# A decoder layer in split fp32: two-term products in three 256-column matmuls, one-operation evictions, and a larger padding tile

## The chip, the cores and the metric

The kernel runs on one core of a Trainium2 chip. The metric is the device time of one execution in microseconds; the time of a kernel is the median of its runs. The engines are TensorE (PE, matmuls; PEld is its weight loads), VectorE (DVE), ScalarE (ACT), GpSimd (POOL) and SyncE (SP, which issues most DMAs).

## What is computed

One layer of a hybrid decoder over 256 tokens of width 2048, all in fp32. In short:

```python
h = rms_norm(x, attn_norm_g)
proj = h @ w_in                                   # 2048 -> 4448 columns
y_rwkv = rwkv7_mixer(token_shift(proj[:3360]))    # 16 heads x 64, recurrent
y_mla = mla_mixer(proj[3360:])                    # 8 heads of latent attention
x = x + concat(y_rwkv, y_mla) @ w_out
h = rms_norm(x, ffn_norm_g)
gate = causal_conv3(h @ w_gate) + conv_b          # 2048 -> 5632
x = x + (silu(gate) * (h @ w_up)) @ w_down        # 5632 -> 2048
return rms_norm(x, final_norm_g)
```

## The kernel before

**Split operands.** TensorE is fed with a rounded format. To come near fp32, each operand is cut into a rounded high part (hi) and what the rounding left over (lo). A product is the sum of three parts: hi x hi, hi x lo and lo x hi. Weights come from memory in pieces of 128 x 1024 fp32. `piece` (L125) issues the DMA of one from SyncE into a tile raw, ScalarE copies it, rounded, into hi (L133), and VectorE subtracts hi from raw into lo (L134). There are three buffers each for raw, hi and lo.

**Two kinds of products.** In `prod_b` (L162) the weights are stationary and the activations stream. The activation tiles, x (four tiles, x_65 to x_68 in the lists below) for the input projection, z for gate and up, cl for the up-projections of the attention, hold for each slice of 128 input channels the high parts of the 256 tokens and behind them their low parts, 512 columns in all. For the eight slices of a piece, one matmul with the high weights runs over all 512 columns (L165): columns 0 to 255 of the accumulator get hi x hi, columns 256 to 511 get the high weights times the low activations. Then eight matmuls with the low weights (L168) add lo x hi into columns 0 to 255. Two pieces fill an accumulator (a tile mm in PSUM, 128 x 512 fp32). In the attention's up-projections a product takes four slices of a piece in place of eight. One call of `prod_b` with eight slices is called a half product below.

In `prod_a` (L178) the activations are stationary and 512 weight columns stream, with three matmuls per slice (L185 to L187). It serves the output projection (stationary tile yhi), the down projection (stationary tiles hh and hl) and the attention's values. The change does not touch it.

**Eviction.** `joined` (L172) empties an accumulator of `prod_b`: ScalarE copies its second half to the destination (L173), VectorE adds the first half (L174), and VectorE multiplies by the row of reciprocal norms, rsB or its like (L175), which the norm has left until then. The destination is h, kraw, gt, up or another tile of the caller.

**Order of the work.** The input projection (35 accumulators of 128 output columns) is mixed with the work of the recurrent mixer: as each pair of accumulators is ready, the kernel appends what depends on them, the gram matrices (pg, L527), transposes (pt, L547), and a triangular solve on VectorE (L578 to L584) that first loads a tile Lp by DMA. Then follow the recurrence in chunks and the attention, the output projection, and from about 466 us to the end the feed-forward layer, in two blocks: for each of 44 column tiles a gate and an up product (L957 to L976), and after each block the down projection. The program order is written by hand, but a scheduler goes over it with an estimate of each instruction's duration and sets the order in each engine's queue. Each engine works through its queue in order. The accumulators mm have three buffers, as have the accumulators ch of the mixer. A tile takes its place in SBUF in the order in which it is allocated; `pad` and `pad2` are tiles that nothing reads.

Of the kernel before, what the change touches and what calls it, by code (L numbers as in the profile page):

```python
# [14 lines left out]
ALU = mybir.AluOpType  # L15
AX = mybir.AxisListType

P = 128
T = 256
# [35 lines left out]
def hybrid_layer(ctx: ExitStack, tc: tile.TileContext, a: dict, out: bass.AP):  # L55
    nc = tc.nc
    V, S, PE = nc.vector, nc.scalar, nc.tensor
# [24 lines left out]
    def hl4(n):  # L82
        return a8(n).rearrange("p (k s) t -> p k s t", s=2)
# [10 lines left out]
    def mm(n="mm"):  # L94
        return ps.tile([P, 512], F32, tag="mm", name=nm(n), bufs=NMM)
# [7 lines left out]
    def con(shape, n, dt=F32):  # L103
        return sb.tile(shape, dt, name=n, bufs=1)
# [2 lines left out]
    nc.gpsimd.memset(pad, 0.0)  # L107
    xT = a["xT"]
    xs_ = [hl4("x") for _ in range(4)]
    pad2 = con([P, 8], "pad2")  # L110
    nc.gpsimd.memset(pad2, 0.0)
    vec = con([P, NVEC], "vec")
    cst = con([P, NCST], "cst")
# [48 lines left out]
    def prod_b(acc, pieces, act, kt0, n, first, last):  # L162
        hi, lo = pieces
        for j in range(n):
            PE.matmul(acc, hi[:, j * P:(j + 1) * P], act(kt0 + j), start=first and j == 0, stop=False,  # L165
                      skip_group_check=True)
        for j in range(n):
            PE.matmul(acc[:, :T], lo[:, j * P:(j + 1) * P], act(kt0 + j)[:, 0, :], start=False,  # L168
                      stop=last and j == n - 1, skip_group_check=True)


    def joined(dst, acc, scale, rows=slice(0, P)):  # L172
        S.copy(dst, acc[rows, T:])  # L173
        V.tensor_tensor(dst, acc[rows, :T], dst, ALU.add)  # L174
        V.tensor_tensor(dst, dst, scale[rows], ALU.mult)  # L175


    def prod_a(accs, pieces, act_hi, act_lo, kt0, n, first, last, tbs=(0, 1)):  # L178
# [12 lines left out]
    def in_tile(i, pf=mm):  # L191
        acc = pf()
        for h in range(2):
            eng = nc.gpsimd if h and 17 <= i < 25 else None
            prod_b(acc, piece(a["win"][i, h], eng=eng), x_hl, h * 8, 8, h == 0, h == 1)
        flush()
        return acc
# [121 lines left out]
    with tc.manual_schedule(engines={mybir.EngineType.SP}):  # L319
        for g in range(4):  # L320
            xsplit(g)
            if g == 0:
                nc.scalar.dma_start(cst, a["cst"])
            if g % 2 == 0:
                for i in range(2):
                    pcs[i, g // 2] = piece(a["win"][wt0[i], g // 2])
            for i in range(2):
                hl = tuple(u[:, (g % 2) * 512:(g % 2 + 1) * 512] for u in pcs[i, g // 2])
                prod_b(acc0[i], hl, x_hl, g * 4, 4, g == 0, g == 3)
        for h in range(2):  # L330
            prod_b(acc0[2], piece(a["win"][26, h]), x_hl, h * 8, 8, h == 0, h == 1)
        sums(0)
        kacc[0] = in_tile(1)
        dve0 = last_lo[0]
        sums(1)
        kacc[1] = in_tile(2, ch)
        rope_tables()
        lora = s4(n="lora")
        nc.sync.dma_start(lora, a["lora"])
# [32 lines left out]
    def shifted(acc, i, rows=slice(0, P), dst=None):  # L372
        h = t1("h", 257)
        nc.gpsimd.memset(h[rows, 0:1], 0.0)
        joined(h[rows, 1:257], acc, rsB, rows)
        o = t1("sh") if dst is None else dst
        S.activation(o[rows], h[rows, 1:257], AF.Copy, scale=om_mu[rows, i:i + 1])
        V.scalar_tensor_tensor(o[rows], h[rows, 0:256], vv("mu", i, rows), o[rows], ALU.mult, ALU.add)
        return o
# [50 lines left out]
    acc = acc0[2]  # L430
    kraw, ksw = t1("kraw"), t1("ksw")
    joined(kraw[0:64], acc, rsB, slice(0, 64))
    shifted(acc, 26, rows=slice(64, 96), dst=sg2)
    sigmoid_(sg2, slice(64, 96))
# [12 lines left out]
    for p in range(8):  # L447
# [4 lines left out]
        acc = kacc[p] if p in kacc else in_tile(1 + p)  # L452
# [45 lines left out]
    for p in range(8):  # L498
        pp, g = p // 2, p % 2
        acc = in_tile(9 + p)  # L500
# [256 lines left out]
    def latent(x, gname, post):  # L757
        c_ = [s4(F32R, "cl").rearrange("p (k s t) -> p k s t", k=2, s=2) for _ in range(2)]
        ssum = t2("css")
        for j in range(4):  # L760
            acc = in_tile(27 + x * 4 + j)
            cr = t2("cr")
            joined(cr, acc, rsB)
            if j == 0:
                S.activation(ssum, cr, AF.Square)
            else:
                sq = t2("csq")
                S.activation(sq, cr, AF.Square)
                V.tensor_tensor(ssum, ssum, sq, ALU.add)
            h_, l_ = (c_[j // 2][:, j % 2, q, :] for q in range(2))  # L770
            S.activation(h_, cr, AF.Copy, scale=vv(gname, j))
            V.scalar_tensor_tensor(l_, cr, vv(gname, j), h_.bitcast(F32), ALU.mult, ALU.subtract)
        pss = at("pss")
        for tb in range(2):
            PE.matmul(pss[:, tb * 2:tb * 2 + 2], ssum[:, tb * P:(tb + 1) * P], ones[:, 0:2], start=True, stop=True)
        m = st("ssm", 2)
        V.tensor_copy(m, pss[:, 0:4:2])
        rr = con([P, 2], f"rr{x}")
        V.tensor_scalar(rr, rsqrt(m, 1.0 / 512, EPS, 2), post, None, ALU.mult)
        rb = con([P, T], f"rrB{x}")  # L780
        bcast(rr, rb, at, t2)
        rrs.append(rr)
        rrB.append(rb)
        cl.append(c_)
# [167 lines left out]
    for blk, nf in enumerate((24, 20)):  # L952
        hh = [s4(F32R, "hh").rearrange("p (k t) -> p k t", k=4) for _ in range(nf // 4)]
        hl = [s4(F32R, "hl").rearrange("p (k t) -> p k t", k=4) for _ in range(nf // 4)]
        for fi in range(nf):
            f = f0 + fi
            accs = []  # L957
            for gu in range(2):
                acc = mm()
# [24 lines left out]
        n = nf // 2  # L984
# [105 lines left out]
```

## Time and profile before

| | |
|---|---|
| Time, median of 3 runs | 1208.7 us (1208.7, 1202.65, 1214.32) |
| Profiled execution: span | 1203.6 us, 18439 instructions (the page has no other time for it) |
| TensorE busy | 1159.9 us (96%) in 6993 matmuls |
| its weight loads | 990.6 us (82%) |
| VectorE busy | 839.1 us (70%) |
| ScalarE busy | 599.4 us (50%) |
| GpSimd busy | 77.4 us (6%) |
| DMA | 215.82 MB, mean 179 GB/s |

The busy times are shares of the span. Matmuls are pipelined and their ends are modelled, so the pace of TensorE is read from the starts of successive matmuls or from long runs of them, not from the busy time. The chain that the profile follows back from the last instruction names what was waited for at each step; windows give the busy time of each engine in a stretch of the span. In both, "L165" is a line of the kernel, an arrow points from what is read to what is written, and "x8" is a count of instructions.

### The profile page before, as it was taken

To read this page: it belongs to the slowest core of one execution; us is meant where nothing else is said; L and a number is where in the kernel's file an instruction comes from. 1 tells how busy PE (TensorE), PEld (TensorE's weight loads), DVE (VectorE), ACT (ScalarE), POOL (GpSimd) and SP (SyncE) were. 2 spreads that over 40 slices of the span, in tenths; PEclk is the share of its full clock that TensorE was granted. 3 is DMA by queue.
4 is the path that set the end of the run, shared out by engine and by line. 5 is a ranking of instruction groups with operands and counts; after the bars stand their busy time and mean duration, and the time that the engine had idled before them with its cause. 6 is when DMAs were issued, how large, how long until landed. Compare 5 with 4: busy or idle time off the path is not lost.

```text
span 1203.6 us, 18439 instructions
## 1 busy us (share of the span) xinstructions
PE 1159.9 (96%) x6993; PEld 990.6 (82%) x6993; DVE 839.1 (70%) x1352; ACT 599.4 (50%) x939; POOL 77.4 (6%) x214
## 2 busy tenths in 40 slices
PE   7899998998799999999999999999999999999996
PEld 6788877887577888888888888888888888888885
DVE  6898749977887556777777776444577777775563
ACT  6784434633444455655555554333455555554442
POOL 1500042002110001000000000000000000000000
PEclk9899998999999999999999999999999999999999
DMA  8555443754133555655555555555655555566662
GB/s 317 177 155 159 138 143 122 213 168 147 62 140 114 184 172 175 206 190 191 187 192 191 191 192 191 193 190 190 200 191 192 192 193 193 192 223 202 205 217 81
DMA packets 71017, 215.82 MB, mean 179 GB/s; under 512 B 17616, under 2 KB 17872, under 8 KB 70928
## 3 DMA queue, kind: packets, MB, share of 16 engines
q1 hardware_dynamic: 69776, 211.84, 53.9%
q10 hardware_dynamic: 768, 2.05, 0.5%
q8 instruction: 55, 0.90, 0.3%
q0 software_dynamic: 384, 0.75, 0.2%
q14 instruction: 34, 0.28, 0.1%
HBM read 210.48 MB, written 3.41 MB: 178 GB/s over the span
## 4 chain that ended last, share of the span: by engine, by line
PE 84%; DVE 8%; DMA 3%; POOL 2%; issue 1%; ACT 1%; SPq 1%; ACTq 0%; DVEq 0%; POOLq 0%
PE mm L165 34%; PE mm L168 17%; PE mm L185 9%; PE mm L187 9%; PE mm L186 9%; DVE lo L134 2%; PE pg L527 1%; DMA xt<-in_x 1%; PE px L677 1%; DMA Lp<-dL 1%; DMA raw<-in_win 0%; POOL cosR L291 0%; DMA dT<-Tq 0%; PE py L677 0%; SPq L540 0%
## 5 line engine op out<-in xcount | busy, mean ns | idle before, releaser
L134 DVE TENSOR_TENSOR lo<-raw,hi 128x1024 fp32r<-128x1024 f32 x368 | 453.0, 1231 | 288.0 <-ACT hi L133 283.1
L133 ACT CAST hi<-raw 128x1024 fp32r<-128x1024 f32 x376 | 395.5, 1052 | 451.7 <-issue 234.9
L165 PE MATMUL mm<-z,hi 128*128 128x512 f32 x1408 | 351.3, 392 | 0.0
L165 PEld LDWEIGHTS mm<-z,hi 128*128 128x128 f32 x1408 | 251.9, 188 | 43.7
L168 PEld LDWEIGHTS mm<-z,lo 128*128 128x128 f32 x1408 | 188.3, 188 | 14.5
L168 PE MATMUL mm<-z,lo 128*128 128x256 f32 x1408 | 191.6, 278 | 0.0
L165 PE MATMUL mm<-x,hi 128*128 128x512 f32 x528 | 144.4, 410 | 17.9 <-DVE h L174 9.6
L186 PE MATMUL mm<-lo,hh 128*128 128x512 f32 x336 | 130.7, 389 | 0.0
L187 PE MATMUL mm<-hi,hl 128*128 128x512 f32 x336 | 130.7, 389 | 0.0
L165 PEld LDWEIGHTS mm<-x,hi 128*128 128x128 f32 x528 | 97.0, 195 | 35.6 <-ACT hi L133 8.3
L185 PE MATMUL mm<-hi,hh 128*128 128x512 f32 x336 | 119.7, 389 | 0.0
L168 PEld LDWEIGHTS mm<-x,lo 128*128 128x128 f32 x528 | 74.7, 193 | 7.4 <-issue 1.0
L168 PE MATMUL mm<-x,lo 128*128 128x256 f32 x528 | 79.9, 288 | 0.0
L186 PEld LDWEIGHTS mm<-lo,hh 128*128 128x128 f32 x336 | 63.1, 188 | 13.1
L187 PEld LDWEIGHTS mm<-hi,hl 128*128 128x128 f32 x336 | 63.1, 188 | 13.1
L185 PEld LDWEIGHTS mm<-hi,hh 128*128 128x128 f32 x336 | 63.1, 188 | 13.0
L186 PE MATMUL mm<-lo,yhi 128*128 128x512 f32 x128 | 51.1, 399 | 0.0
L187 PE MATMUL mm<-hi,ylo 128*128 128x512 f32 x128 | 50.5, 394 | 0.0
L185 PE MATMUL mm<-hi,yhi 128*128 128x512 f32 x128 | 49.6, 405 | 0.0
L964 POOL MEMSET gt<- 128x2 f32 x44 | 4.3, 100 | 575.8 <-DVE hl L976 558.9
L187 PEld LDWEIGHTS mm<-hi,ylo 128*128 128x128 f32 x128 | 24.1, 188 | 5.6 <-DVE ylo L749 0.4
L185 PEld LDWEIGHTS mm<-hi,yhi 128*128 128x128 f32 x128 | 23.9, 188 | 5.7 <-DVE kn L174 0.8
(291 smaller groups left out, 1142.8 us busy)
## 6 DMA issues: line engine op xcount, KB each, us to landing
raw<-in_wgu SPq DMA_DIRECT2D x176, 512.0 KB, 3.3
raw<-in_wdn SPq DMA_DIRECT2D x88, 512.0 KB, 4.1
raw<-in_win SPq DMA_DIRECT2D x70, 512.0 KB, 3.7
raw<-in_wout SPq DMA_DIRECT2D x32, 512.0 KB, 3.4
raw<-in_wuq SPq DMA_DIRECT2D x6, 512.0 KB, 3.3
xraw<-in_xT SPq DMA_DIRECT2D x4, 512.0 KB, 6.3
xt<-in_x SPq DMA_DIRECT2D x4, 512.0 KB, 6.7
raw<-in_wuv SPq DMA_DIRECT2D x4, 512.0 KB, 3.3
```

The lines of the kernel that those rows point to most:

```text
L133: S.copy(hi, raw)
L134: sub = (eng or V).tensor_tensor(lo, raw, hi.bitcast(F32), ALU.subtract).ins
L165: PE.matmul(acc, hi[:, j * P:(j + 1) * P], act(kt0 + j), start=first and j == 0, stop=False, skip_group_check=True)
L168: PE.matmul(acc[:, :T], lo[:, j * P:(j + 1) * P], act(kt0 + j)[:, 0, :], start=False, stop=last and j == n - 1, skip_group_check=True)
L185: PE.matmul(accs[tb], ah, wh, start=first and j == 0, stop=False)
L186: PE.matmul(accs[tb], ah, wl, start=False, stop=False)
L187: PE.matmul(accs[tb], al, wh, start=False, stop=last and j == n - 1)
L527: PE.matmul(pg[h][:, o:o + P], BK[pp][hs, gg, w * 2 + r, :, :], AR[pp][hs, gg, w * 2 + r, :, :], start=o == 0, stop=True, skip_group_check ...
L677: PE.matmul(dst[HS[h], a_ * 64:(a_ + 1) * 64], lhsT, rhs, start=n == 0 and a_ == 0, stop=True, skip_group_check=True)
L964: nc.gpsimd.memset(gt[:, 0:2], 0.0)
```

## The change

`prod_b` now runs two matmuls of 256 columns for each slice with the high weights, one over the high and one over the low activations, and both add into columns 0 to 255, as the matmuls with the low weights do. The same high weights are thus loaded twice. `joined` has one operation left: VectorE multiplies the accumulator by the reciprocal norms into the destination. There are 144 such evictions, 88 of them of gate and up. `pad2` grows from 8 to 88 fp32 per partition, from 32 to 352 bytes: each tile that is allocated after it moves by 320 bytes, while the x tiles (whose buffers z uses later) and `pad` stay. The two products of a slice carry no `skip_group_check` any more, which is no instruction.

```diff
-    pad2 = con([P, 8], "pad2")
+    pad2 = con([P, 88], "pad2")
...
         for j in range(n):
-            PE.matmul(acc, hi[:, j * P:(j + 1) * P], act(kt0 + j), start=first and j == 0, stop=False,
-                      skip_group_check=True)
+            for s in range(2):
+                PE.matmul(acc[:, :T], hi[:, j * P:(j + 1) * P], act(kt0 + j)[:, s, :],
+                          start=first and j == 0 and s == 0, stop=False)
         for j in range(n):
             PE.matmul(acc[:, :T], lo[:, j * P:(j + 1) * P], act(kt0 + j)[:, 0, :], start=False,
-                      stop=last and j == n - 1, skip_group_check=True)
+                      stop=last and j == n - 1)
...
     def joined(dst, acc, scale, rows=slice(0, P)):
-        S.copy(dst, acc[rows, T:])
-        V.tensor_tensor(dst, acc[rows, :T], dst, ALU.add)
-        V.tensor_tensor(dst, dst, scale[rows], ALU.mult)
+        V.tensor_tensor(dst, acc[rows, :T], scale[rows], ALU.mult)
```

Lines behind the eviction thus stand one line higher than before, and the two loops of `prod_b` one lower (L166 and L169). In the lists below a row is a run of like instructions in an engine's queue: line, operation, tile written, tiles read, shape and count.

TensorE, one half product of an accumulator of gate and up and the next one, before:

```order
L165 MATMUL mm_5616<-z_4387,hi_5641 128x512 x4
L165 MATMUL mm_5616<-z_4388,hi_5641 128x512 x4
L168 MATMUL mm_5616<-z_4387,lo_5642 128x256 x4
L168 MATMUL mm_5616<-z_4388,lo_5642 128x256 x4
L165 MATMUL mm_5678<-z_4385,hi_5681 128x512 x4
L165 MATMUL mm_5678<-z_4386,hi_5681 128x512 x4
L168 MATMUL mm_5678<-z_4385,lo_5682 128x256 x4
L168 MATMUL mm_5678<-z_4386,lo_5682 128x256 x4
```

The same place on TensorE after the change:

```order
L166 MATMUL mm_6221<-z_4915,hi_6254 128x256 x8
L166 MATMUL mm_6221<-z_4916,hi_6254 128x256 x8
L169 MATMUL mm_6221<-z_4915,lo_6255 128x256 x4
L169 MATMUL mm_6221<-z_4916,lo_6255 128x256 x4
L166 MATMUL mm_6295<-z_4913,hi_6298 128x256 x8
L166 MATMUL mm_6295<-z_4914,hi_6298 128x256 x8
L169 MATMUL mm_6295<-z_4913,lo_6299 128x256 x4
L169 MATMUL mm_6295<-z_4914,lo_6299 128x256 x4
```

A half product is 24 matmuls of 256 columns where it was 8 of 512 and 8 of 256; nothing else stands between them.

VectorE at the beginning of the solve (about 178 us in the profile before; Lp is the solve's matrix, Mp its mask, Tq its result, tm a temporary, h the destination of an eviction), before:

```order
L134 TENSOR_TENSOR lo_2040<-raw_2037,hi_2039 128x1024
L134 TENSOR_TENSOR lo_2093<-raw_2090,hi_2092 128x1024
L578 TENSOR_TENSOR Lp_1766<-Lp_1766,Mp 128x1024
L582 TENSOR_TENSOR tm_1822<-Tq_1821,Lp_1766 128x31
L584 TENSOR_TENSOR Tq_1821<-Tq_1821,tm_1822 128x31
L174 TENSOR_TENSOR h_1904<-mm_1776,h_1904 128x256
L582 TENSOR_TENSOR tm_1822<-Tq_1821,Lp_1766 128x60
L175 TENSOR_TENSOR h_1904<-h_1904,rsB 128x256
```

The same place on VectorE after the change:

```order
L134 TENSOR_TENSOR lo_2284<-raw_2281,hi_2283 128x1024
L577 TENSOR_TENSOR Lp_2046<-Lp_2046,Mp 128x1024
L134 TENSOR_TENSOR lo_2360<-raw_2357,hi_2359 128x1024
L581 TENSOR_TENSOR tm_2116<-Tq_2115,Lp_2046 128x31
L174 TENSOR_TENSOR h_2198<-mm_2054,rsB 128x256
L583 TENSOR_TENSOR Tq_2115<-Tq_2115,tm_2116 128x31
L174 TENSOR_TENSOR h_2274<-mm_2213,rsB 128x256
```

The solve's first multiply stands one split (lo) earlier, and the next eviction follows it behind that split, one operation long.

TensorE between the last matmul of the gram matrices and the accumulator that waits at that place (pv are transposes of the mixer), before:

```order
L165 MATMUL mm_1974<-x_66,hi_1977 128x512 x4
L168 MATMUL mm_1974<-x_65,lo_1978 128x256 x4
L168 MATMUL mm_1974<-x_66,lo_1978 128x256 x4
L165 MATMUL mm_1974<-x_67,hi_1999 128x512
L615 MATMUL pv_1912<-cst,sh_1773 128x128 x2
L165 MATMUL mm_1974<-x_67,hi_1999 128x512 x3
L165 MATMUL mm_1974<-x_68,hi_1999 128x512 x4
L168 MATMUL mm_1974<-x_67,lo_2000 128x256 x4
L168 MATMUL mm_1974<-x_68,lo_2000 128x256 x4
L165 MATMUL mm_2036<-x_65,hi_2039 128x512 x4
```

The same place on TensorE after the change:

```order
L614 MATMUL pv_2204<-cst,sh_2051 128x128 x2
L166 MATMUL mm_2213<-x_65,hi_2216 128x256 x8
L166 MATMUL mm_2213<-x_66,hi_2216 128x256 x8
L169 MATMUL mm_2213<-x_65,lo_2217 128x256 x4
L169 MATMUL mm_2213<-x_66,lo_2217 128x256 x4
L166 MATMUL mm_2213<-x_67,hi_2246 128x256 x8
L166 MATMUL mm_2213<-x_68,hi_2246 128x256 x8
L169 MATMUL mm_2213<-x_67,lo_2247 128x256 x4
L169 MATMUL mm_2213<-x_68,lo_2247 128x256 x4
L166 MATMUL mm_2280<-x_65,hi_2283 128x256 x8
L166 MATMUL mm_2280<-x_66,hi_2283 128x256 x8
L169 MATMUL mm_2280<-x_65,lo_2284 128x256 x4
```

Ahead of the waiting accumulator (mm_2036 before, mm_2356 after) stand the second half of mm_1921 and all of mm_1974 before, and the rest of mm_2054 and all of mm_2213 and mm_2280 after.

## The prediction

> **What bounds the kernel now.** First the page's span and busy times, then the chain that ended last (its line by engine and its line by source line).
>
> ```profile
> span 1203.6 us, 18439 instructions
> PE 1159.9 (96%) x6993; PEld 990.6 (82%) x6993; DVE 839.1 (70%) x1352; ACT 599.4 (50%) x939; POOL 77.4 (6%) x214
> PE 84%; DVE 8%; DMA 3%; POOL 2%; issue 1%; ACT 1%; SPq 1%; ACTq 0%; DVEq 0%; POOLq 0%
> PE mm L165 34%; PE mm L168 17%; PE mm L185 9%; PE mm L187 9%; PE mm L186 9%; DVE lo L134 2%; PE pg L527 1%; DMA xt<-in_x 1%; PE px L677 1%; DMA Lp<-dL 1%; DMA raw<-in_win 0%; POOL cosR L291 0%; DMA dT<-Tq 0%; PE py L677 0%; SPq L540 0%
> ```
>
> TensorE carries 84% of the chain, and L165 and L168, the two lines that the change rewrites, half of it. VectorE carries 8%. Busy time by stage says where:
>
> ```profile
> core 0: us, PE busy (x) PEld busy (x) DVE busy (x) ACT busy (x) POOL busy (x), PEclk, DMA share, GB/s
> 40.00:50.00 10.00, 7.41 (x25) 6.27 (x26) 7.05 (x14) 6.77 (x13) 8.06 (x25) 0.66 0.52 163
> 50.00:88.00 38.00, 37.55 (x222) 31.21 (x221) 37.29 (x84) 33.35 (x63) 1.31 (x10) 1.00 0.48 142
> 178.00:200.00 22.00, 15.99 (x82) 13.71 (x82) 18.68 (x39) 11.50 (x23) 5.06 (x5) 0.84 0.39 138
> 265.00:375.00 110.00, 95.58 (x957) 76.39 (x956) 89.60 (x166) 46.52 (x99) 17.29 (x46) 0.98 0.31 107
> 466.00:1180.00 714.00, 714.00 (x3832) 616.85 (x3831) 477.78 (x651) 357.04 (x508) 8.87 (x58) 1.00 0.59 194
> ```
>
> From 466 us on (gate, up and down) TensorE is never idle and VectorE has a third of its time free: an eviction saved there is worth nothing, a nanosecond per matmul everything. VectorE is nearly full from 50 to 88 us, and TensorE loses time at 40 to 50, 178 to 200 and 265 to 375 us.
>
> **The change, part 1: three matmuls of 256 columns for one of 512 and one of 256.** The chain in the gate/up stage, in order of time, gives the pace:
>
> ```profile
> 695.18 1.83 PE mm L165 x8
> 697.01 0.94 PE mm L168 x8
> 697.96 1.83 PE mm L165 x8
> 699.79 0.91 PE mm L168 x8
> ...
> 706.21 1.83 PE mm L165 x8
> ```
>
> Four half products (8 matmuls of L165 and 8 of L168 each) take 706.21 - 695.18 = 11.03 us, 2.7575 us each. There are 176 (1408 matmuls of L165 on z, by eights). Each becomes 24 matmuls of 256 columns, so all depends on the pace of those. A 512-column matmul takes 1.83/8 = 229 ns. A 256-column one takes 0.91/8 = 114 or 0.94/8 = 117.5 ns, in turns. Two halves thus cost 228 to 235 ns: the second load of the high half buys and costs almost nothing beside a full stream. Whether it is made at all, lines 185 and 186 tell: there one stationary operand (yhi or hh) serves two matmuls in a row, and both have their weight load.
>
> ```profile
> L186 PEld LDWEIGHTS mm<-lo,hh 128*128 128x128 f32 x336 | 63.1, 188 | 13.1
> L185 PEld LDWEIGHTS mm<-hi,hh 128*128 128x128 f32 x336 | 63.1, 188 | 13.0
> ```
>
> Which pace will a long run take? The padding tile moves every tile behind x and z by 320 bytes. In the built program x and z begin 160 bytes past a multiple of 512, hi and lo 352 bytes past one; after the change all of them are at 160. Now only the up-projections (tile cl, at 352 as hi and lo are) read both operands from the same offset. Their 256-column runs are four long:
>
> ```profile
> 315.58 1.09 PE L165 MATMUL mm<-cl,hi 128*128 128x512 f32 x4
> 316.50 0.64 PE L168 MATMUL mm<-cl,lo 128*128 128x256 f32 x4
> 316.98 1.09 PE L165 MATMUL mm<-cl,hi 128*128 128x512 f32 x4
> ...
> 329.65 0.63 PE L168 MATMUL mm<-cl,lo 128*128 128x256 f32 x4
> 330.12 1.08 PE L165 MATMUL mm<-cl,hi 128*128 128x512 f32 x4
> ```
>
> By starts, four take 316.98 - 316.50 = 0.48 and 330.12 - 329.65 = 0.47 us, in the mean 118.75 ns each, slower than either pace on z. I take this, since it is the only row with the placement that z will have. A half product then takes 24 x 118.75 ns = 2.850 us, +0.0925 us; x176 = **+16.3 us**. The bounds are the fastest and slowest rows: 24 x 0.91/8 = 2.730 us, -4.8 us in all, and 24 x 0.48/4 = 2.880 us, +21.6 us.
>
> [...]
>
> The input projection has 70 half products on x, which in the stage where TensorE waits least take
>
> ```profile
> 104.97 0.94 PE mm L168 x8
> 105.91 1.84 PE mm L165 x8
> 107.75 0.94 PE mm L168 x8
> ```
>
> 107.75 - 104.97 = 2.78 us. At 2.850 that is +0.07 us each. Some 14 of them run between 40 and 88 us, where VectorE's full queue hides it; 56 x 0.07 = **+3.9 us** (-2.8 to +5.6 by the same bounds; all 70 if that cover is gone, +1). The 20 up-projection products go from 316.98 - 315.58 = 1.40 to 12 x 118.75 = 1.425 us: **+0.5 us** (-0.7 to +0.8).
>
> **Part 2: the padding and the 512-column matmuls that stay.** In the output projection's second half the stationary tile yhi stands at 160 and hi and lo at 352; in the down projection hh stands at 352 like them.
>
> ```profile
> 447.38 0.39 PE L186 MATMUL mm<-lo,yhi 128*128 128x512 f32 x1
> ...
> 448.54 0.39 PE L185 MATMUL mm<-hi,yhi 128*128 128x512 f32 x1
> 789.63 0.39 PE L186 MATMUL mm<-lo,hh 128*128 128x512 f32 x1
> ...
> 790.76 0.62 PE L185 MATMUL mm<-hi,hh 128*128 128x512 f32 x2
> ```
>
> Five steps take 1.16 and 1.13 us: 232 against 226 ns. With all at 160, the 192 matmuls of that half should step at 226: **-1.2 us** (0 if offset is not the reason).
>
> **Part 3: one operation per eviction.** joined loses a copy on ScalarE and an add on VectorE, 144 times:
>
> ```profile
> L174 DVE TENSOR_TENSOR gt<-mm,gt 128x256 f32<-128x256 f32 x44 | 18.4, 419 | 0.0
> L173 ACT COPY gt<-mm 128x256 f32<-128x256 f32 x44 | 16.1, 367 | 0.0
> ```
>
> The 88 of gate and up are hidden under TensorE: nothing. The weight DMAs stay as many, and their queue has room (DMA share 0.59 from 466 us on). Elsewhere:
>
> - 40 to 88 us: 10 adds of 0.42 us, 4.2 us of a full VectorE queue. I take **-3** (0 to -4.2): TensorE, 37.55 of 38 us busy behind it, is late next.
> - The wait at 178 us. VectorE's queue holds the solve's first multiply (line 578), which waits for a DMA, ahead of the eviction that frees the accumulator. First the chain, then TensorE's rows:
>
> ```profile
> 175.82 6.07 DMA Lp<-dL
> 181.92 1.24 DVE Lp L578
> 183.66 0.34 DVE h L174
> 177.32 0.73 PE L168 MATMUL mm<-x,lo 128*128 128x256 f32 x5
> 184.05 3.78 PE L165 MATMUL mm<-x,hi 128*128 128x512 f32 x8 [6.01 <-DVE h L174]
> ```
>
>  In the new order two whole tiles and most of a third stand between the last gram matmul and the blocked tile, where one and three quarters stood: some 6 us more to do. But VectorE now has a split (lo, 1.23 us) between that multiply and the eviction. And behind the 6.01 us of idling eight matmuls took 3.78 us in place of 1.83, at a granted clock of 0.84. So 6 - 6 + 1.2 leaves a wait of 1 to 2 us and no lost clock. I take **-5** (+1.2 if only the split counts, -8 with all the clock's 2 us).
> - 265 to 375 us: 22 adds, 9.2 us of VectorE's 89.6. TensorE lacks 14.4 us there, partly to chains without an eviction (the scan, group norm). I take **-4** (0 to -9.2).
>
> [...]
>
> **Sum.** 16.3 + 3.9 + 0.5 - 1.2 - 3 - 5 - 4 = +7.5 us on the profiled span of 1203.6, 1211.1 us. The page has no other time for that execution; the median of the runs, 1208.7, lies 5.1 us above its span. With it the forecast is **1216 us**, +0.6%. About 1% (12 us) is what a measurement of this kernel can tell from no change.
>
> **The rivals.**
>
> - *The run locks at the fast pace.* z's rows hold 0.91 for eight matmuls on end, every second time; without a 512-column run to throw them off, they may all do so. For it: eight are a longer run than four. Against it: z's offset then is not z's offset now. -4.8 - 2.8 - 0.7 - 1.2 - 12 = -21.5: **1187 us**.
> - *The paces go on in turns,* (0.91 + 0.94)/16 = 115.6 ns, 2.775 us: +3.1 us, 0 in front, -1.2 - 12: **1199 us**.
> - *The weight load becomes the bound* (the slower side). With 256 columns there is one load per 119 ns or so; if loads slow each other, matmuls follow the loads. The place is the 176 half products of gate and up. By the 0.48 us row (120 ns): 21.6 + 5.6 + 0.8 - 1.2 - 12 = +14.8: **1224 us**. It decides from 119.5 ns: 5800 matmuls of 256 columns outside the hidden stage, 0.8 ns more each, are the 4.6 us that separate 1216 from 1% slower.
> - *The evictions bring nothing,* because each place waits for a chain with no joined in it (the DMA of Lp, ScalarE, the scan). The copies and adds go, and the change's purpose with them: 7.5 + 12 = +19.5: **1228 us**.
>
> **How the numbers follow.** Forecast 38%, fast lock 30%, paces in turns 5%, load-bound 15%, evictions worth nothing 12%. Below 1196.6 us lies the fast lock: faster 30%. Forecast and turns: same 43%. The last two: slower 27%. Both outer cases are needed to leave out no more than 2 in 10, with the nearer half of what stays unknown in each: the evictions may bring up to 4.2 + 8 + 9.2 = 21.4 us in place of 12, half of the rest is 4.7, so the fast lock reaches down to 1182; in the load-bound case they may bring half of 12, 1230. The range is **1182 to 1230**. The forecast's own range is 1207 (evictions at 21.4 us) to 1228 (evictions at nothing).
>
> **What would show it.** In gate and up, TensorE without idle time and a chain of 24 matmuls in 2.85 us (2.73 for the fast lock, 2.88 for the load-bound case). At 178 us a wait under 3 us and eight products after it at full clock. VectorE some 60 us less busy, ScalarE 50. The forecast is wrong if the pace is off by 2 ns (11.6 us over 5800 matmuls), or if a new order of instructions makes a wait that the old trace doesn't have.

## The result and the profile after

The changed kernel takes 1221.5 us (median of 6 runs, 1221.1 to 1223.4) and the kernel before 1210.4 us (6 runs, 1202.7 to 1215.9): 1.0093 times as long, with a 95% interval of 1.007 to 1.0116. The change costs 11.1 us. The forecast of 1216 had it 5.5 us too low. The runs were taken in several series, and in each the median of the kernel before was 1209.3 to 1210.9 us, so that times are compared across them. One run of the variant with a distance of 256 bytes, 1450.7 us at a granted clock of 0.75, is left out everywhere.

The page of the changed kernel, its span, busy times and chain:

```profile
span 1220.0 us, 22236 instructions
PE 1187.6 (97%) x9041; PEld 1108.8 (91%) x9041; DVE 777.1 (64%) x1208; ACT 564.1 (46%) x795; POOL 76.6 (6%) x214
PE 93%; DVE 3%; DMA 1%; issue 1%; SPq 0%; POOL 0%; ACT 0%; ACTq 0%; POOLq 0%
PE mm L166 39%; PE mm L169 19%; PE mm L184 9%; PE mm L185 9%; PE mm L186 9%; PE pg L526 1%; PE px L676 1%; DMA raw<-in_win 1%; DVE Tq L583 1%; PE py L676 1%; DMA Lp<-dL 0%; PE pT L640 0%; SPq L539 0%; PE pS L676 0%; PE at L166 0%
```

VectorE's share of the chain fell from 8% to 3% and its busy time by 62 us, ScalarE's by 35 (50 were forecast). TensorE's busy time rose by 28. So VectorE holds the end up less, and TensorE works longer. Where, the starts of the matmuls with the high weights on z tell, first of the kernel before, then of the changed one (duration min/median/max in ns, then first and last start in us):

```profile
L165 PE MATMUL mm<-z,hi x1408: 388/392/482, 467.6 to 1083.6; 128*128 128x512 f32 x176
```

```profile
L166 PE MATMUL mm<-z,hi x2816: 277/283/364, 461.9 to 1099.6; 128*128 128x256 f32 x188
```

The stage now begins 5.7 us earlier and lasts 637.7 us, where it lasted 616.0 (the first down projection, 130.7 us in both, lies within): 21.7 us more. The chain in the changed kernel shows how:

```profile
664.05 0.96 PE mm L169 x8
665.01 1.92 PE mm L166 x16
...
681.33 0.96 PE mm L169 x8
```

Six half products take 681.33 - 664.05 = 17.28 us, 2.880 each or 120.0 ns per matmul, without a second pace: 8 take 0.96 every time. Before, a half product took 2.7575 us. 176 x 0.1225 = 21.6 us: the whole loss of this stage is this one number.

The gain ahead of it, by the windows of the changed kernel that answer to those of before:

```profile
40.00:50.00 10.00, 7.57 (x48) 7.10 (x49) 4.93 (x12) 6.10 (x11) 8.60 (x30) 0.83 0.49 144
50.00:88.00 38.00, 38.00 (x307) 36.43 (x306) 37.82 (x83) 31.93 (x60) 0.79 (x8) 1.00 0.42 137
178.00:200.00 22.00, 17.76 (x136) 17.33 (x135) 21.38 (x42) 10.53 (x18) 6.28 (x7) 0.92 0.44 142
265.00:375.00 110.00, 103.85 (x1081) 88.15 (x1080) 88.06 (x151) 44.02 (x83) 16.67 (x46) 0.98 0.39 126
```

TensorE idles 6.2 us from 265 to 375 where it idled 14.4, and 4.2 us from 178 to 200 where it idled 6.0. In the two windows at 40 to 88 us it idles 2.4 us, where it idled 3.0. The windows are the same stretches of time in both kernels, so the work in them is not quite the same.

On the two profiled executions the balance is 16.4 us, on the medians 11.1: the profiled execution of before lies at the quick end of that kernel's runs. (In every other profiled execution the time is 1.8 us above the span, which would make it some 1205.4 us, an estimate.) The medians are used for times below, the profiles for what happens within a stage.

### The profile page after: what moved, and what is told of

Read it like the earlier page. It is cut to its first block, busy times and chain, and to the rows that moved or that the text cites. A ratio compares the mean times of both kernels' runs of the same rounds, so it can differ in the third digit from the quotient of the medians.

```text
span 1220.0 us, 22236 instructions
## 1 busy us (share of the span) xinstructions
PE 1187.6 (97%) x9041; PEld 1108.8 (91%) x9041; DVE 777.1 (64%) x1208; ACT 564.1 (46%) x795; POOL 76.6 (6%) x214
## 3 DMA queue, kind: packets, MB, share of 16 engines
q8 instruction: 71, 1.16, 0.4%
## 4 chain that ended last, share of the span: by engine, by line
PE 93%; DVE 3%; DMA 1%; issue 1%; SPq 0%; POOL 0%; ACT 0%; ACTq 0%; POOLq 0%
PE mm L166 39%; PE mm L169 19%; PE mm L184 9%; PE mm L185 9%; PE mm L186 9%; PE pg L526 1%; PE px L676 1%; DMA raw<-in_win 1%; DVE Tq L583 1%; PE py L676 1%; DMA Lp<-dL 0%; PE pT L640 0%; SPq L539 0%; PE pS L676 0%; PE at L166 0%
## 5 line engine op out<-in xcount | busy, mean ns | idle before, releaser
L166 PE MATMUL mm<-z,hi 128*128 128x256 f32 x2816 | 367.8, 283 | 0.0
L166 PEld LDWEIGHTS mm<-z,hi 128*128 128x128 f32 x2816 | 351.1, 192 | 0.2
L169 PE MATMUL mm<-z,lo 128*128 128x256 f32 x1408 | 198.2, 283 | 0.0
L169 PEld LDWEIGHTS mm<-z,lo 128*128 128x128 f32 x1408 | 181.9, 192 | 0.0
L166 PE MATMUL mm<-x,hi 128*128 128x256 f32 x1056 | 151.8, 292 | 11.1 <-ACT hi L133 8.1
L166 PEld LDWEIGHTS mm<-x,hi 128*128 128x128 f32 x1056 | 137.9, 197 | 14.0 <-ACT hi L133 8.1
L185 PE MATMUL mm<-lo,hh 128*128 128x512 f32 x336 | 130.7, 389 | 0.0
L186 PE MATMUL mm<-hi,hl 128*128 128x512 f32 x336 | 130.7, 389 | 0.0
L169 PE MATMUL mm<-x,lo 128*128 128x256 f32 x528 | 78.4, 289 | 0.0
L169 PEld LDWEIGHTS mm<-x,lo 128*128 128x128 f32 x528 | 70.8, 197 | 0.1
L174 DVE TENSOR_TENSOR up<-mm,rs2B 128x256 f32<-128x256 f32 x44 | 18.7, 425 | 62.0 <-PE mm L169 62.0
L174 DVE TENSOR_TENSOR gt<-mm,rs2B 128x256 f32<-128x256 f32 x44 | 18.7, 425 | 49.4 <-PE mm L169 49.4
```

The costliest lines, as they stand in the source:

```text
L166: PE.matmul(acc[:, :T], hi[:, j * P:(j + 1) * P], act(kt0 + j)[:, s, :], start=first and j == 0 and s == 0, stop=False)
L174: V.tensor_tensor(dst, acc[rows, :T], scale[rows], ALU.mult)
L185: PE.matmul(accs[tb], ah, wl, start=False, stop=False)
L186: PE.matmul(accs[tb], al, wh, start=False, stop=last and j == n - 1)
```

## The experiments

Three things set the kernels apart: (a) the three matmuls of 256 columns, (b) the distance between weights and activations that the padding sets, and (c) the evictions. Kernels that differ in a padding alone have in their traces the same matmuls on x, z and cl, and the same operations on VectorE and ScalarE, in the same order.

### The padding undone, and the padding alone

```diff
 (changed kernel)
-    pad2 = con([P, 88], "pad2")
+    pad2 = con([P, 8], "pad2")
```

> The change with its padding undone (pad2 of 32 bytes, so the weights hi and lo start 352 bytes past a multiple of 512 and x and z 160), products and evictions new. Theory A (placement: the pace of 120 ns per 256-column matmul comes from weights and activations that start at the same offset): the runs of 256 columns on z go back to the 113 to 118 ns of before, 24 matmuls in 2.72 to 2.83 us, and the time falls by 8 to 28 us from the changed kernel's 1221.5, to 1193 to 1213 us. Theory B (the weight load is the bound: one load for each 256 columns cannot be faster than 120 ns): 120 ns stays, 1219 to 1224 us.

Measured: 1212.2 us (12 runs), 1.0025 of before (1.0007 to 1.0042). The matmuls on z, and the chain:

```profile
L166 PE MATMUL mm<-z,hi x2816: 278/280/368, 458.8 to 1087.1; 128*128 128x256 f32 x188
```

```profile
665.66 0.94 PE mm L169 x8
666.60 1.88 PE mm L166 x16
...
682.62 0.94 PE mm L169 x8
```

The stage lasts 628.3 us, 9.4 less than with the padding, and the time is 9.3 less. Six half products take 16.96 us, 117.8 ns per matmul. Loads are still about as many as matmuls (310 and 312 from 50 to 88 us). So 120 ns is no limit of the load that holds in every placement (theory B falls), and placement sets 2.2 ns of it. But 113 doesn't come back either: 117.8 is about the slower one (0.94 us for eight) of the two paces that the kernel before had in turns. At the old placement, three matmuls of 256 columns cost 628.3 - 616.0 = 12.3 us more than one of 512 and one of 256.

The same profile has a control. The tile cl of the up-projections is allocated behind `pad2` like hi and lo, so that its distance from them stays 0 with either padding. One product of them:

```profile
319.71 0.96 PE mm L166 x8
320.67 0.48 PE mm L169 x4
321.15 0.86 PE pgate L738 x2
```

Its 12 matmuls still take 321.15 - 319.71 = 1.44 us, 120.0 ns each. The padding changed the pace on z, where it changed the distance (120.0 to 117.8 ns), and not on cl, where it did not.

```diff
 (kernel before)
-    pad2 = con([P, 8], "pad2")
+    pad2 = con([P, 88], "pad2")
```

> The kernel before with the padding alone (pad2 of 352 bytes: hi and lo at the offset of x and z). Theory A (placement): the 256-column matmuls on z, eight in a row, slow from 113 to 118 ns to 120, the 512-column ones to 230 to 240; the stage of 176 half products takes 5 to 16 us more, the time is 1213 to 1226 us. Theory B (weight load): a 512-column matmul hides its load in any placement; the pace stays at 229 and 113 to 118 ns, and the output projection's second half gains 1 us: 1207 to 1211 us.

Measured: 1214.5 us (12 runs) beside 1209.6, 1.0034 (1.0014 to 1.0054).

```profile
L165 PE MATMUL mm<-z,hi x1408: 388/390/477, 474.7 to 1096.9; 128*128 128x512 f32 x176
```

```profile
665.09 0.95 PE mm L168 x8
666.05 1.84 PE mm L165 x8
...
681.85 0.95 PE mm L168 x8
```

The stage lasts 622.2 us, 6.2 more, at 2.793 us per half product. The padding costs the old products too, and most of it in those of 256 columns: eight take 0.95 us every time, where they took 0.91 and 0.94 in turns, and eight of 512 take 1.84 where they took 1.83. Less 1.2 us that the output projection gains (below), that agrees with the 4.9 us between the medians. Theory A holds; that 512 columns would not feel the placement (B) is wrong.

### What the evictions are worth

```diff
 (changed kernel)
     def joined(dst, acc, scale, rows=slice(0, P)):
-        V.tensor_tensor(dst, acc[rows, :T], scale[rows], ALU.mult)
+        S.activation(dst, acc[rows, :T], AF.Copy, scale=0.0)
+        V.tensor_tensor(dst, acc[rows, :T], dst, ALU.add)
+        V.tensor_tensor(dst, dst, scale[rows], ALU.mult)
```

> The changed kernel with an eviction of three operations again: ScalarE writes zeros (a copy with scale 0), VectorE adds the accumulator and multiplies. The result is the same; only the cost of the 144 evictions comes back. If the shorter evictions are worth the 12 us that the prediction gave them: 1231 to 1236 us, the loss before 466 us. If they are worth 5 us, as the two spans suggest (16.4 us in all where the pace of gate and up alone explains 21.5): 1225 to 1228. If nothing: 1221. In gate and up 120 ns and no idle time in each case.

Measured: 1229.1 us (4 runs, 1227.1 to 1232.4), 1.0162 of before (1.0134 to 1.019), that is 7.6 us over the changed kernel.

```profile
L166 PE MATMUL mm<-z,hi x2816: 277/283/365, 472.6 to 1110.3; 128*128 128x256 f32 x188
```

The stage lasts 637.7 us as in the changed kernel: 88 evictions with two operations more change nothing there. It begins 10.7 us later (in an execution that was the slowest of the four). So by this run the short eviction is worth some 8 us, none of it in gate and up, between the expectations of 5 and 12. This eviction brings its own order of instructions with it, as the change did; the 7.6 us include that.

### Each part where it pays

```diff
 (changed kernel, pad2 of 32 bytes)
-    def prod_b(acc, pieces, act, kt0, n, first, last):
+    def prod_b(acc, pieces, act, kt0, n, first, last, wide=False):
...
+            if wide:
+                PE.matmul(acc, hi[:, j * P:(j + 1) * P], act(kt0 + j), start=first and j == 0, stop=False,
+                          skip_group_check=True)
+                continue
             for s in range(2):
...
+        if wide:
+            S.copy(dst, acc[rows, T:])
+            V.tensor_tensor(dst, acc[rows, :T], dst, ALU.add)
+            V.tensor_tensor(dst, dst, scale[rows], ALU.mult)
+            return
...
-                    prod_b(acc, piece(a["wgu"][f, gu, h]), z_hl, h * 8, 8, h == 0, h == 1)
+                    prod_b(acc, piece(a["wgu"][f, gu, h]), z_hl, h * 8, 8, h == 0, h == 1, True)
...
-            joined(up, accs[1], rs2B)
+            joined(up, accs[1], rs2B, wide=True)
```

> A mixture, with pad2 of 32 bytes: gate and up (176 half products) as in the kernel before, matmuls of 512 and 256 columns and the three-operation eviction; the input projection and the up-projections as in the changed kernel, with the one-operation eviction. If the evictions are worth something only ahead of 466 us and the new products cost where TensorE is never idle (theory of two opposite terms), it keeps the gain and sheds the loss: half products of gate and up back to 2.75 to 2.77 us from 2.827 in the run with the padding undone, 176 x 0.07 = 12 us less than its 1212.2: 1198 to 1202 us. If the gain of the evictions lay in gate and up (rival), nothing is kept there: 1207 to 1212 us.

Measured: 1201.0 us (6 runs, 1200.0 to 1202.8) beside 1209.5, 0.9935 (0.9914 to 0.9957). It beats both kernels: the one before by 8.5 us, the changed one by 20.5, as expected (1198 to 1202).

```profile
L166 PE MATMUL mm<-z,hi x1408: 387/392/482, 462.8 to 1078.8; 128*128 128x512 f32 x176
```

The stage is back at 616.0 us to the tenth, and it begins 4.8 us earlier than before. The gain of the evictions and most of the loss of the products lie in different stages and can be had apart.

### Which distance

The distance is that from the beginning of x or z to that of hi or lo, modulo 512 bytes. Four single-parameter variants of the changed kernel:

```diff
-    pad2 = con([P, 88], "pad2")
+    pad2 = con([P, 24], "pad2")   # or 16, 32, 40
```

> The changed kernel with pad2 of 96 bytes: hi and lo start 256 bytes away from x and z modulo 512. Theory A (placement): if only the same offset modulo 512 is slow, 113 to 118 ns and 1193 to 1213 us; if the same offset modulo 256 is what counts, 120 ns and 1219 to 1224. Theory B (weight load): 120 ns, 1219 to 1224 us.

> The changed kernel with pad2 of 64 bytes: the weights hi and lo start 224 bytes away from x and z modulo 512 (96 modulo 128). So far 0 and 256 bytes gave 120.0 ns per 256-column matmul in gate and up, 192 bytes 117.8. Theory A1 (the distance modulo 128 sets the pace, 0 being slow): a third value, between 113 and 119 ns. Theory A2 (only the distances 0 modulo 256 are slow): 117.8 ns.

> The changed kernel with pad2 of 128 bytes: distance 288 bytes (32 modulo 128 and modulo 256). Theory A1 (distance modulo 128): not 120 ns, and if the effect is symmetric the same pace as with distance 224 (96 modulo 128). Theory A2 (0 modulo 256 alone is slow): 117.8 ns.

> The changed kernel with pad2 of 160 bytes: a distance of 320 bytes, 64 modulo 128 and modulo 256, where 192 bytes is 64 modulo 128 and 192 modulo 256. If the distance modulo 128 sets the pace: 117.8 ns per 256-column matmul, gate and up 498.6 us together, 1209 to 1213 us, as at 192. If the distance modulo 256 does: another pace (it has been 120.0 at 0, 118.4 at 32, 117.8 at 192 and 116.6 at 224).

Matmuls on z with 24, 16, 32 and 40 fp32 of padding:

```profile
L166 PE MATMUL mm<-z,hi x2816: 278/283/365, 462.4 to 1100.0; 128*128 128x256 f32 x188
```

```profile
L166 PE MATMUL mm<-z,hi x2816: 277/280/367, 459.6 to 1083.3; 128*128 128x256 f32 x188
```

```profile
L166 PE MATMUL mm<-z,hi x2816: 277/281/367, 461.6 to 1092.2; 128*128 128x256 f32 x188
```

```profile
L166 PE MATMUL mm<-z,hi x2816: 276/281/366, 463.5 to 1091.6; 128*128 128x256 f32 x188
```

| Distance, bytes (modulo 128) | Stage, us | ns per matmul on z | Time, us |
|---|---|---|---|
| 0 (0), the change | 637.7 | 120.0 | 1221.5 |
| 256 (0) | 637.6 | 120.0 | 1222.2 |
| 288 (32) | 630.6 | 118.3 | 1214.7 (one run) |
| 192 (64), e1 | 628.3 | 117.8 | 1212.2 |
| 320 (64) | 628.1 | 117.8 | 1214.1 (one run) |
| 224 (96) | 623.7 | 116.6 | 1205.8 (one run) |

The ns are those of six half products in the chain (256: of one). On z the two pairs that are equal modulo 128 have equal paces, 0 and 256 bytes and 192 and 320 (theory A1; that 0 modulo 256 alone is slow, A2, falls with 224 and 288). The effect is not symmetric: 32 and 96 differ by 1.7 ns. The time at 320 bytes, 1214.1 us, lies above the 1209 to 1213 that were expected of it. At 0 modulo 128 nearly every matmul follows the one before at 119 to 121 ns and at 64 at 116 to 119; at 96 and 32 the steps go from 113 to 120 and from 115 to 123 ns. The timed run at 256 bytes confirms the change's own: 1.0102 of before (1.0073 to 1.0132).

The input projection does not bear the rule out. Its matmuls on x are 256 columns wide in the changed kernel, its variants and the mixtures alike. At 0 bytes one of its half products takes 104.92 - 102.04 = 2.88 us, at 256 bytes 2.88 too, at 192 bytes 103.32 - 100.49 = 2.83 us. First the mixture with 384 bytes (0 modulo 128, below; the lines of its products are L170 and L173), then the changed kernel with 320 (64 modulo 128):

```profile
100.74 0.95 PE mm L173 x8
101.69 1.90 PE mm L170 x16
103.59 0.95 PE mm L173 x8
```

```profile
100.61 0.91 PE mm L169 x8
101.51 1.81 PE mm L166 x16
103.33 0.91 PE mm L169 x8
```

At 384 bytes it takes 2.85 us, 118.8 ns per matmul, and not 120.0. At 320 some take 2.72 us, 113.3 ns, which no half product of 256 columns alone reached on z in the mean. With the distance the pace changed, on x from 113.3 ns at 320 bytes to 120.0 at 0, but a rule modulo 128 is not shown.

```diff
 (changed kernel, pad2 of 32 bytes)
-    pad = con([P, 8], "pad")
+    pad = con([P, 16], "pad")
```

> The changed kernel with pad2 of 32 bytes and the first tile, pad, of 64: all of x, z and the weights move by 32 bytes, and the distance stays 192. If the distance alone counts: 117.8 ns as in the run with the padding undone. If the position in a line of 64 bytes counts (now 0, 32 in all runs before): another pace.

```profile
L166 PE MATMUL mm<-z,hi x2816: 278/279/367, 460.7 to 1089.0; 128*128 128x256 f32 x188
```

Measured: 1211.3 us (one run), a stage of 628.3 us, as with the same distance 32 bytes lower. Moving x, z and the weights together by 32 bytes changes nothing; other common shifts were not tried.

Does the best distance help the mixture too? And what about 384 bytes, 0 modulo 128?

```diff
 (mixture)
-    pad2 = con([P, 8], "pad2")
+    pad2 = con([P, 16], "pad2")   # or 56
```

> The mixture (old products and evictions in gate and up, new ones elsewhere) with pad2 of 64 bytes, a distance of 224 bytes between weights and activations in place of 192. The long runs of 256 columns went from 117.8 to 116.6 ns with it. If the distance acts on the 512-column matmuls as on those of 256 (theory: one conflict behind both), a half product of gate and up falls below 2.757 us, by up to 0.03, and the time to 1195 to 1200 us from 1201. If a stream of 512 columns doesn't feel the distance: 1200 to 1201.5 us, of which the input projection gives less than 1.

> The mixture with pad2 of 224 bytes: a distance of 384 bytes (128 modulo 256, 0 modulo 128). If the pace goes by the distance modulo 128 (0 slow): the input projection's 256-column matmuls at 120.0 ns, gate and up as slow as in the kernel before with the large padding (230.8 and 119.0 ns), 1203 to 1208 us. If modulo 256, with 0 slow and 128 the farthest from it: 113 to 118 ns and 1194 to 1201 us.

With 224 bytes, then with 384:

```profile
L166 PE MATMUL mm<-z,hi x1408: 392/396/481, 463.1 to 1087.8; 128*128 128x512 f32 x176
```

```profile
L166 PE MATMUL mm<-z,hi x1408: 387/393/482, 461.1 to 1086.4; 128*128 128x512 f32 x176
```

Both expectations missed. At 224 bytes the stage of 512 and 256 columns lasts 624.7 us, 8.7 more than at 192, and the kernel takes 1208.6 us (12 runs; 0.9984 of before, 0.9966 to 1.0002); the best distance for 256 columns alone is a bad one here. At 384 bytes it lasts 625.3 us (1208.6, one run), where 0, likewise 0 modulo 128, gave 622.2. For streams that change between 512 and 256 columns the paces follow no rule modulo 128 either, and of the four distances tried the one of before, 192, is the best.

### Is the second load of the same weights special?

```diff
 (changed kernel, pad2 of 32 bytes)
-        for j in range(n):
-            for s in range(2):
+        for s in range(2):
+            for j in range(n):
```

> New products with pad2 of 32 bytes (117.8 ns), and the loops of prod_b exchanged: all eight slices of the high weights over the high activations, then all eight again over the low ones, so that the same weights are never loaded twice in a row. If the second load of the same weights is an ordinary load (the prediction's reading): 117 to 118.5 ns, 1209 to 1214 us. If loading the tile that is in use already is cheaper or dearer: another pace in the matmuls of L166 than the 117.8 ns of L169.

```profile
L166 PE MATMUL mm<-z,hi x2816: 278/279/368, 460.1 to 1088.5; 128*128 128x256 f32 x188
```

Measured: 1210.8 us (one run), a stage of 628.4 us. With each tile loaded twice in a row it was 628.3. In this stream, loading the tile that is in use cost as much as loading another.

## Why the prediction was right or wrong

**The pace (failed step).** The prediction took 118.75 ns, the mean of two runs of four matmuls on cl, for all matmuls on z: +16.3 us. It is 120.0 ns, and the term 21.6. Gate and up cost 5.3 us more than forecast; all else, 11.1 - 21.6 = -10.5 us on the medians, came out 1.7 us better than the forecast's 3.9 + 0.5 - 1.2 - 12 = -8.8; and the median of before, with more runs, is 1.7 us higher than the 1208.7 that the forecast started from. 5.3 - 1.7 + 1.7 is the distance from 1216.2, the sum before rounding, to 1221.5. That all else came out so near is in part luck: ahead of gate and up the pace was mis-sized in the same way, 5.6 + 0.8 us in place of 3.9 + 0.5 (a half product on x takes 2.88 us), and what the evictions and the new order brought made up for it. The choice of row was right: it was taken for its equal offset, and undoing that offset gives 117.8 on z, while cl, whose offset stays equal, keeps 120.0. What failed was its resolution. The two runs, 0.48 and 0.47 us, are 120 and 117.5 ns; they are read to 0.01 us and each begins behind 512 columns. A mean over them was no estimate of a pace that eight in a row hold without a change. The upper bound, 120, was the value.

**Where the loss comes from.** The prediction held that two matmuls of 256 columns cost almost nothing beside one of 512, and took the slower pace for the work of the placement. The runs divide the 21.7 us: 12.3 for the split at the old placement, where all 24 matmuls go at about the slower of the two old paces, and 9.4 for the padding. The split as such, the larger part, is no term of the forecast; the rival with the paces in turns gives it 3.1 us.

**The padding.** In the output projection's second half the predicted row came out, at the place where the offset became equal:

```profile
448.06 0.39 PE L186 MATMUL mm<-hi,ylo 128*128 128x512 f32 x1
...
449.19 0.39 PE L186 MATMUL mm<-hi,ylo 128*128 128x512 f32 x1
```

Five steps take 1.13 us, 226 ns, where they took 1.16. An equal offset went with the faster pace there, where 512 weight columns stream past a stationary activation (226 ns where it was 232), and with the slower one where z streams (120.0 ns where the old offset gave 117.8). The prediction gave the padding as -1.2 us; it is that and +9.4.

**The evictions.** -12 us were forecast. The third experiment gives 7.6, with an order of its own. The balance asks for more: of the -10.5 us above, -1.2 are the padding's, and if the matmuls ahead of gate and up cost 5.6 + 0.8 us, -15.7 are left. In the mixture, whose half products on x take 2.82 us where they took 2.78, it is 8.5 + 2.2 + 0.8 = 11.5. So the evictions with their new order are worth some 8 to 16 us, an estimate from these runs, which do not narrow it further. For the two profiles, this view of the first 375 us (the sum row) of before and after gives 34.0 and 22.1 us of idle TensorE:

```profile
sum 375.00, PE 341.03 PEld 288.02 DVE 300.58 ACT 193.30 POOL 68.49; mean PE 48.72 PEld 41.15 DVE 42.94 ACT 27.61 POOL 9.78
```

```profile
sum 375.00, PE 352.91 PEld 330.51 DVE 283.80 ACT 180.10 POOL 68.53; mean PE 50.42 PEld 47.22 DVE 40.54 ACT 25.73 POOL 9.79
```

11.9 us less, but in other places: 8.3 from 265 to 375 us, where 4 were forecast (near the bound of 9.2), 1.8 at 178 to 200 instead of 5, and 0.6 at 40 to 88 instead of 3. From 50 to 88 us VectorE stays full (37.82 of 38 us) with the adds gone: other work moved up into the time that they left, of the splits only 0.85 us (13.38 where it was 12.53).

**The wait at 178 us.** The wait that the prediction knew went as reasoned; two others came behind it. VectorE after, and TensorE's two waits:

```profile
174.22 1.23 DVE L577 TENSOR_TENSOR Lp<-Lp,Mp 128x1024 f32<-128x1024 f32 x1 [6.13 <-DMA Lp<-dL]
175.36 1.22 DVE L134 TENSOR_TENSOR lo<-raw,hi 128x1024 fp32r<-128x1024 f32 x1
176.59 0.42 DVE L174 TENSOR_TENSOR h<-mm,rsB 128x256 f32<-128x256 f32 x1
...
192.42 2.55 DVE L583 TENSOR_TENSOR Tq<-Tq,tm 128x240 f32<-128x240 f32 x1
194.90 0.47 DVE L377 SCALAR_TENSOR_TENSOR sh<-h,vec,sh 128x256 f32<-128x256 f32 x1
```

```profile
180.87 0.44 PE L614 MATMUL pv<-cst,sh 128*128 128x128 f32 x2 [1.43 <-DVE sh L377]
195.52 0.41 PE L614 MATMUL pv<-cst,sh 128*128 128x128 f32 x2 [2.81 <-DVE sh L377]
```

VectorE waits 6.13 us for the same DMA and TensorE works on through it, since the order gave it enough to do. Then it waits twice for transposes whose input stands in VectorE's queue among the solve's steps, 4.2 us in all. The clock was saved only in part: from 178 to 200 us it is 0.92 in the mean, where it was 0.84, but behind the second wait it is 0.67 and then 0.82 for 6.5 us, where full clock was forecast.

```profile
192.20:195.50 3.30, 0.51 (x5) 0.31 (x4) 3.30 (x4) 0.91 (x1) 2.50 (x2) 1.00 0.52 159
195.50:199.00 3.50, 3.48 (x21) 3.50 (x22) 3.36 (x8) 1.11 (x2) 0.00 (x0) 0.67 0.49 154
199.00:202.00 3.00, 3.00 (x23) 3.00 (x23) 2.97 (x4) 0.40 (x2) 2.14 (x1) 0.82 0.54 175
```

The prediction counted the wait of the tile that it knew, and asked for VectorE's queue only at its head. Its "no lost clock" behind a wait of 1 to 2 us was the author's estimate, and no run shows that such a wait keeps full clock whenever it comes. In the changed kernel the wait of 1.43 us at 180.87 was followed by a clock of 1.00 to 192.2 us; the one of 2.81 us, in a stretch of 3.30 us with 0.51 us of work, was followed by 0.67 and 0.82. Nor does the length of a wait alone decide it in these runs: in the kernel before, one of 2.13 us, at 321.59, was followed by a clock of 1.00 to 329 us; in the changed kernel the clock was 0.50 from 246 to 250 us, and the longest wait from 236 us on was 0.62 us. So the forecast's wait of 1 to 2 us was no warrant of full clock.

**The rivals.** The fast lock and the paces in turns fell: in no kernel with 256 columns alone did a half product of gate and up take under 2.80 us in the mean. The fast pace exists all the same, on x at 320 bytes. The load-bound rival had the pace, 120 ns, but as a bound on loads in any placement it falls, since the same number of loads go at 116.6 to 117.8 with another padding; whether the distance slows the loads or the streams, no run here separates. That the evictions bring nothing fell with the third experiment and the mixture.

**The chances.** The likeliest case was a time within 1% of before (43%), slower by over 1% had 27%. The time is 0.93% over before, and its interval leaves no doubt of the sign, which the forecast of +0.6% had without claiming it. The sum of two opposite terms of 20 and 12 us was always going to be decided by the pace's last nanosecond, as the prediction's own warning (2 ns is 11.6 us) says.

## What to carry to other kernels

Where TensorE never idles, read the pace of a matmul form from the chain over many in a row, and take the ends of short runs as bounds and not their mean: 1 ns is 4 us here. Apply a change stage by stage: here fewer eviction operations paid ahead of 466 us, where VectorE's queue held TensorE up (7.6 us in the third experiment), fewer and wider matmuls paid in gate and up, where TensorE never idles (616.0 us in place of 628.3), and a kernel may do both (1201.0 us). And when a tile's size changes, look at what moves behind it: 320 bytes of padding cost 9.3 us here, about as much as the shorter evictions saved in the third experiment.

## What was not expected of the hardware

The pace of a stream of matmuls without a gap changed with the distance in SBUF between the stationary and the moving operand: from 116.6 ns at 224 bytes to 120.0 at 0 for 256 columns on z, in the same order of instructions, each over 4224 matmuls. What in the chip makes it so, no run here shows. Open is also why the mixed stream of 512 and 256 columns was fastest at another distance (192 bytes, a stage of 616.0 us) than 256 columns alone (224 bytes, 623.7 us), and why x and z differ at 320 (113.3 and 117.8 ns).
